# Turning q and k on VectorE in 32x32 blocks, with x2 kept by every fourth column

## Chip, cores and metric

The kernel runs on one core of one Trainium2 chip. The metric is the device time of one execution in microseconds (us); lower is better. Of the kernel before there are three times, 2680.54, 2680.54 and 2683.51 us; their median is 2680.54 us.

## The reference, cut to what matters

Two layers over 2048 tokens of width 1024, all in float32. Layer A normalises x, projects it to [u | z], pools u over 2, 4, 8 or 16 trailing tokens, maps and gates it, projects it back, and adds a gated embedding; its result is called x2 below. From x2 come the shared keys and values, and layer B's queries and gate:

```python
kv_in = rms_norm(x, kv_norm)
k_all, v_all = jnp.split(kv_in @ w_kv, 2, axis=-1)
k_sh = rms_norm(split_heads(k_all), k_norm)       # 16 heads of 64
v_sh = split_heads(v_all)
h = rms_norm(x, b_norm[j])
q, z = jnp.split(h @ b_w_in[j], 2, axis=-1)
q = rms_norm(split_heads(q), b_q_norm[j])
o = stick_breaking_attention(q, k_sh, v_sh)
x = x + (o * jax.nn.silu(z)) @ b_w_out[j]
```

For a query t and an earlier key s the weight is `beta[t,s] * prod_{s<j<t} (1 - beta[t,j])` with `beta = sigmoid(q.k / 8)`; only keys before t count. The kernel uses that the weights are differences of a running product, so it multiplies the running product with differences of neighbouring values, v[t-1] - v[t].

## The kernel before, in words

Every float32 operand of a product is split into a high and a low part, and a product is three matmuls: high x high, high x low, low x high. The stream is kept with channels on the 128 partitions and tokens in the free dimension, in four chunks of 512 tokens (`NSUB`, `W5`).

**First stage** (lines 219 to 865). For each chunk 22 steps run in a written order (`steps`, L757 on): four times z and u of layer A (`run_z`, `run_u`), four output steps (`run_o`), four gate steps (`run_g`), and then two steps each for q, k and v (`run_kvq`, eight heads a step). Each step also fetches the weights two steps ahead and converts those of the next step (`Weights.fetch`, `Weights.convert`: high part on ScalarE L148, low part on VectorE L149). `run_g` makes x2 and its two parts with `split` (L589), stores both in DRAM, and squares x2 on ScalarE (L596); the sum of squares gives, by a matmul with a column of ones (L625), the norm of each token.

A q, k or v step has two halves of two token tiles (128 tokens each). In `run_kvq` x2 is the stationary operand, so the result (L614) has tokens on the partitions and eight heads in the free dimension. `keyed` scales it and takes each head's norm (ScalarE L710, L712, VectorE L714, GpSimd L80, L81); `normed` applies the norm (VectorE L722). When all four token tiles are done, four closures `finish(m)`, one for a pair of heads, are appended to `lag` and run in the next step, at the last k-tile of its first half (L618): four TensorE transposes against the identity (L731) bring a pair to channels on the partitions, in PSUM; ScalarE and VectorE split it (L737, or with the gain of q and k L739, L740), and one DMA stores it as `kd` or `qd` (L742).

For v, `token_major` makes a copy moved down by one partition with DMAs issued on ScalarE's queue (L664 to L674), since the token before lies on the partition before; the first row comes from the tile before, or from the chunk before through `ve`. `differences` subtracts on GpSimd (L691), splits, and stores to `vd` (L698). For the last chunk's second v step the DMAs go out on SyncE, and this work runs inside the attention (`early`).

`tc.keep_in_program_order` (named `stay` in places) fixes an instruction's place on its engine; `queue` (L88) does that for stores and loads on SyncE's queue; functions in `pend` run at the third k-tile of the next product (`stored_late`). Tiles come from pools with a fixed number of buffers: for example `t4` has four, shared by `hl`, `vv` and the kept weights.

**Second stage** (from L868): attention, last chunk first, one head after another, over key chunks from the last to the first ("slots"; `slots` L1211). In a slot TensorE multiplies q and k (`front`, L936, L937: two matmuls, of q as (high, low) and of q as (low, high) with the two parts of k below each other), ScalarE takes the sigmoid (L940), VectorE scans (L945, L948), TensorE turns the result (`turn`, L961), ScalarE and VectorE split it (L964, L965), and TensorE multiplies with v (`gather`, L973, L974). The loads of a slot (`load_q`, `load_k`, `load_v`) are issued one slot ahead (`begin(i + 1)`, L1253). In between, single matmuls of other work are laid into TensorE's order as fillers, their number a slot from a small estimate of VectorE's and TensorE's times (`shares`): during the last chunk's attention the gates z of all chunks (`gate_z`, whose products are scaled on VectorE by L1057), later the output projections (`post`).

Of the kernel before, what the change touches and what calls it, by code (L numbers as in the profile page):

```python
# [15 lines left out]
P = 128  # L16
# [19 lines left out]
def trunk_kernel(ctx, tc, x, xt, pt0, wut, cols, heads, zin, grp, aout, agate, aple,  # L36
# [22 lines left out]
    gqk = cp.tile([P, 1], F32, name="gqk")  # L59
# [7 lines left out]
    qd = [[dram.tile([P, 2, W5], F32, name=f"qd{s}_{m}") for m in range(NH // 2)] for s in range(NSUB)]  # L67
    kd = [[dram.tile([P, 2, W5], F32, name=f"kd{s}_{m}") for m in range(NH // 2)] for s in range(NSUB)]
    vd = [[dram.tile([8, P, 4, P], F32, name=f"vd{s}_{b}") for b in range(2)] for s in range(NSUB)]
# [116 lines left out]

    def load_q(c, h):
        qa = io.tile([P, W5], F32R, tag="io", name="qa")
        qb = io.tile([P, W5], F32R, tag="io", name="qb")
        rows = qd[c][h // 2][h % 2 * HD : (h % 2 + 1) * HD]  # L190
        for l in range(2):
            nc.sync.dma_start(out=f(qa)[l * HD : (l + 1) * HD], in_=rows[:, l])
            nc.sync.dma_start(out=f(qb)[(1 - l) * HD : (2 - l) * HD], in_=rows[:, l])
        return qa, qb

    def load_k(kc, h):
        kk = io.tile([P, W5], F32R, tag="io", name="kk")
        rows = kd[kc][h // 2][h % 2 * HD : (h % 2 + 1) * HD]
        for l in range(2):
            nc.sync.dma_start(out=f(kk)[l * HD : (l + 1) * HD], in_=rows[:, l])  # L200
        return kk

    def load_v(kc, h):
        vv = io.tile([P, 4, P], F32R, tag="io", name="vv")
        nc.sync.dma_start(out=f(vv), in_=vd[kc][h // 8][h % 8])
        return vv
# [12 lines left out]
    with ExitStack() as st:  # L219
# [17 lines left out]
        hp = st.enter_context(tc.tile_pool(name="hp", bufs=1))  # L237
        halo = [[hp.tile([P, HALO], F32, name=f"halo{o}_{i}") for i in range(2)] for o in range(KT)]
# [15 lines left out]
        def split(pr, src, lo):  # L254
            A.copy(out=pr[:, 0], in_=src)
            lo.tensor_tensor(out=pr[:, 1], in0=src, in1=f(pr[:, 0]), op=ALU.subtract)

# [234 lines left out]
        def run_u(s, g, wu):  # L492
# [7 lines left out]
            for k in range(2):  # L500
                o = 2 * g + k
                ub = t2.tile([P, HALO + W5], F32, tag="ub", name="ub", bufs=2)
# [3 lines left out]
                cur, lo, sh = ub, 0, 1  # L506
                while sh < win:
                    nx = t2.tile([P, HALO + W5], F32, tag="us", name="us", bufs=2)
# [62 lines left out]
        def run_g(s, b, wg, wl):  # L571
# [13 lines left out]
            for k in range(2):  # L585
# [3 lines left out]
                split(pr, t, V)  # L589
# [3 lines left out]
            for k in range(2):  # L593
                o, t = 2 * b + k, ts[k]
                sq = tmp("sq")
                A.activation(out=sq, in_=t, func=AF.Square)  # L596
# [6 lines left out]
        def run_kvq(s, kind, b, ws):  # L603
            ck = chunk[s]
            for j0 in (0, 2):
# [25 lines left out]
                fins = [token_major(s, kind, b, j0 + i, pss2[i]) for i in range(2)]  # L631
# [16 lines left out]
        def token_major(s, kind, b, j, ps):  # L648
            tk = slice(j * P, (j + 1) * P)
            rj = chunk[s]["r2"][:, j : j + 1]  # L650
            ps8 = ps.rearrange("q (h d) -> q h d", d=HD)
            if kind == "v":

                if s == NSUB - 1 and b:
                    both = f(pair("vl"))
                    vr, vs = (both[:, e].rearrange("q (h d) -> q h d", d=HD) for e in range(2))
                else:
                    vr = t2.tile([P, 8, HD], F32, tag="tmp", name="vr", bufs=8)
                    vs = t2.tile([P, 8, HD], F32, tag="qn", name="vs", bufs=5)
                A.activation(out=vr, in_=ps8, func=AF.Identity, scale=rj)  # L660
                last = s == NSUB - 1 and b
                start = nc.sync.dma_start if last else nc.scalar.dma_start
                prev, chunk[s]["vr"] = chunk[s].get("vr"), vr
                start(out=ve[s][b][j : j + 1], in_=vr.rearrange("q h d -> q (h d)")[P - 1 : P])  # L664

                def shifted(stay=lambda ins: ins):
# [673 lines left out]
```

## Time and profile before

| | |
|---|---|
| median of three times | 2680.54 us |
| time of the profiled execution's span (first to last instruction) | 2679.3 us |
| VectorE, ScalarE, GpSimd busy | 71%, 52%, 35% |
| DMA | 590 MB, 220 GB/s on average |
| q1, the queue of SyncE: share of the 16 DMA engines' span | 65.3% |
| TensorE clock granted | 1.000 |

The profiled execution's own time is its span of 2679.3 us and about 1.2 us around it, 2680.5 us. PE is TensorE's matmul row, PEld its weight loads, DVE is VectorE, ACT ScalarE, POOL GpSimd, SP SyncE. A row "out<-in" names tiles by the program's names; a mean time of a matmul is longer than the distance to the next one, since matmuls are pipelined. A line number is that of the listing above.

### The profile page before, as it was taken

The numbers are of one execution on the slowest core, as the hardware profiler recorded it, in microseconds if no ns is written. First come the engines' busy times: TensorE is split into PE (matmuls) and PEld (weight loads), VectorE is DVE, ScalarE is ACT, GpSimd is POOL, SyncE is SP. The second block draws the span as 40 slices with busy tenths as digits, with TensorE's granted clock in tenths as the row PEclk, the third lists the DMA queues.
The fourth block names the chain that finished last, engine by engine and source line by source line (L and its number), as shares of the span: only waits on it lengthen the run. The fifth ranks groups of instructions, "written<-read, shape, count | busy, mean of one in ns | idle before, by whom it ended". The sixth has DMA issues, their size and how long they took to land.

```text
span 2679.3 us, 39424 instructions
## 1 busy us (share of the span) xinstructions
PE 2668.1 (100%) x13358; PEld 2229.9 (83%) x13358; DVE 1911.5 (71%) x2474; ACT 1397.2 (52%) x2735; POOL 927.7 (35%) x740
## 2 busy tenths in 40 slices
PE   9999999999999999999999999999999999999999
PEld 7888888888888888888888888888888888888887
DVE  6776625665266643665399999999999998886632
ACT  6455623455135551345356666666666666665531
POOL 2675337643486434853221111122111221212220
PEclk9999999999999999999999999999999999999999
DMA  8657795567856678543679665556766677778975
GB/s 327 222 175 271 251 308 188 192 240 251 303 175 226 232 259 298 168 151 134 223 236 286 195 220 176 166 172 191 211 199 177 185 222 227 201 209 261 267 237 177
DMA packets 281366, 590.00 MB, mean 220 GB/s; under 512 B 33702, under 2 KB 67750, under 8 KB 281164
## 3 DMA queue, kind: packets, MB, share of 16 engines
q1 hardware_dynamic: 270818, 571.41, 65.3%
q0 software_dynamic: 4608, 8.39, 1.9%
q10 hardware_dynamic: 5738, 7.68, 1.0%
q8 instruction: 106, 1.74, 0.3%
q14 instruction: 96, 0.79, 0.1%
HBM read 438.40 MB, written 136.38 MB: 215 GB/s over the span
## 4 chain that ended last, share of the span: by engine, by line
PE 97%; DVE 1%; DMA 0%; issue 0%; ACT 0%; SPq 0%; ACTq 0%; DVEq 0%
PE psd L614 19%; PE psd L168 9%; PE psd L167 9%; PE psd L166 9%; PE psa L961 9%; PE psd L1023 6%; PE psd L1025 6%; PE psd L1027 6%; PE pso L974 5%; PE psl L937 5%; PE pso L973 5%; PE psl L936 5%; PE pst L731 1%; PE psdt L1023 1%; PE psdt L1025 1%; PE psdt L1027 1%
## 5 line engine op out<-in xcount | busy, mean ns | idle before, releaser
L614 PE MATMUL psd<-wpair,x 128*128 128x512 f32 x2304 | 536.8, 391 | 0.0
L948 DVE TENSOR_TENSOR_SCAN pp<-kap,pp,zeros 128x512 f32<-128x512 f32 x384 | 513.5, 1339 | 7.7 <-ACT kap L940 7.0
L964 ACT CAST at<-psa 128x512 fp32r<-128x512 f32 (+3 forms) x640 | 325.7, 523 | 348.6 <-PE psa L961 338.1
L614 PEld LDWEIGHTS psd<-wpair,x 128*128 128x128 f32 x2304 | 429.9, 188 | 87.0
L965 DVE TENSOR_TENSOR at<-psa,at 128x512 fp32r<-128x512 f32 (+3 forms) x640 | 375.1, 598 | 62.0 <-ACT at L964 57.5
L940 ACT ACTIVATE kap<-psl 128x512 f32<-128x512 f32 (+3 forms) x640 | 345.7, 540 | 94.0 <-PE psl L937 90.6
L961 PE MATMUL psa<-ident,pp 128*128 128x128 f32 x2176 | 329.4, 273 | 2.0 <-DVE at L965 1.5
L961 PEld LDWEIGHTS psa<-ident,pp 128*128 128x128 f32 x2176 | 263.6, 140 | 58.2 <-DVE at L965 4.2
L936 PE MATMUL psl<-kk,qa 128*128 128x512 f32 (+3 forms) x640 | 275.1, 430 | 0.5 <-ACT at L964 0.5
L945 DVE TENSOR_TENSOR_SCAN pp<-kap,ahead 128x128 f32<-128x128 f32 (+3 forms) x256 | 224.3, 878 | 40.1 <-ACT kap L940 38.7
L974 PE MATMUL pso<-at,vv 128*128 128x512 f32 (+3 forms) x640 | 234.0, 366 | 0.0
L937 PE MATMUL psl<-kk,qb 128*128 128x512 f32 (+3 forms) x640 | 232.9, 364 | 0.0
L973 PE MATMUL pso<-at,vv 128*128 128x512 f32 (+3 forms) x640 | 232.3, 363 | 0.0
L167 PE MATMUL psd<-xp,wpair 128*128 128x512 f32 x512 | 199.5, 390 | 2.0 <-DVE xp L316 2.0
L166 PE MATMUL psd<-xp,wpair 128*128 128x512 f32 x512 | 199.8, 391 | 1.1 <-ACT xp L315 1.1
L168 PE MATMUL psd<-xp,wpair 128*128 128x512 f32 x512 | 199.3, 390 | 0.0
L149 DVE SCALAR_TENSOR_TENSOR wpair<-wraw,gains,wpair 128x512 fp32r<-128x512 f32 x192 | 161.7, 883 | 46.1 <-ACT wpair L148 45.6
L143 POOL TENSOR_TENSOR wpair<-wraw,wpair 128x512 fp32r<-128x512 f32 x99 | 145.5, 1479 | 82.0 <-ACT wpair L141 78.1
L148 ACT ACTIVATE wpair<-wraw,gains 128x512 fp32r<-128x512 f32 x192 | 132.9, 718 | 64.2 <-DMA wraw<-in_bq_dram 25.9
L141 ACT CAST wpair<-wraw 128x512 fp32r<-128x512 f32 x148 | 89.9, 618 | 121.4 <-PE psd L168 87.5
L1062 POOL TENSOR_TENSOR zr<-zr,sgz 128x512 f32<-128x512 f32 x32 | 61.6, 1924 | 257.3 <-ACT sgz L1061 233.8
L974 PEld LDWEIGHTS pso<-at,vv 128*128 128x128 f32 x640 | 120.2, 188 | 26.3
(207 smaller groups left out, 5338.9 us busy)
## 6 DMA issues: line engine op xcount, KB each, us to landing
kk<-kd SPq DMA_DIRECT2D x320, 128.0 KB
vv<-vd SPq DMA_DIRECT2D x160, 256.0 KB
wraw<-in_kv_dram SPq DMA_DIRECT2D x128, 256.0 KB
wpair<-wzd SPq DMA_DIRECT2D x64, 512.0 KB
wpair<-wod SPq DMA_DIRECT2D x64, 512.0 KB
wpair<-wgd SPq DMA_DIRECT2D x64, 512.0 KB
wpair<-wu SPq DMA_DIRECT2D x48, 512.0 KB
wpair<-wi SPq DMA_DIRECT2D x36, 512.0 KB
```

What stands on the lines that cost most here:

```text
L166: T.matmul(ps, wst(units, kt, 0, c0), acts[kt][:, 0], start=(begin and kt == order[0]), stop=False)
L167: T.matmul(ps, wst(units, kt, 0, c0), acts[kt][:, 1], start=False, stop=False)
L168: T.matmul(ps, wst(units, kt, 1, c0), acts[kt][:, 0], start=False, stop=(end and kt == order[-1]))
L614: T.matmul(pss2[i], ck["x2"][kt][:, xh, tk], wst(ws, kt, wh, 0, W5), start=(kt == 0 and xh == 0 and wh == 0), stop=(kt == KT - 1 and wh == 1))
L936: T.matmul(ps[:, :w], qa[:, qs], kk[:, :w], start=True, stop=False)
L937: T.matmul(ps[:, :w], qb[:, qs], kk[:, :w], start=False, stop=True)
L940: A.activation(out=kp[:, r0:], in_=ps[:, :w], func=AF.Sigmoid, scale=-1.0)
L948: V.tensor_tensor_scan(out=pp[:, ::-1], data0=kp[:, ::-1], data1=zeros.to_broadcast([P, W5]), initial=st["carry"][j], op0=ALU.mult, op1=AL ...
L961: T.transpose(pt[:, j * P : (j + 1) * P], pp[:, r0 + kt * P : r0 + (kt + 1) * P], ident)
L965: V.tensor_tensor(out=at[:, 1, cs], in0=pt[:, cs], in1=f(at[:, 0, cs]), op=ALU.subtract)
L973: T.matmul(po[:, cs], vv[:, kt, :], at[:, 0, cs], start=(st["diag"] and kt == 0), stop=False)
L974: T.matmul(po[:, cs], vv[:, kt, :], at[:, 1, cs], start=False, stop=(st["last"] and kt == 3))
```

## The change

Four things, which belong together:

- **x2 by fours.** `run_g` writes the parts of x2 with every fourth column together (`by_four`): column j*128 + t of the tile is token 4t + j. A token tile j of a q, k or v step then holds tokens j, 4 + j, 8 + j and so on, one per partition. The square of x2 is permuted alike. The gate z undoes the order when it is scaled (L1057), and x2 itself is stored as before.
- **Block transposes.** `normed` scales in place and then lets VectorE turn each 32x32 block of the tile (`V.transpose`) into a buffer `blocks`, written with a step of four elements. A quadrant of 32 partitions then holds 128 consecutive tokens, and the partition in it is a channel of 32. The four TensorE transposes of `finish` go; the split reads `blocks` in SBUF. `blocks` shares its memory with the pooling's work tiles, which become one tile `work`.
- **Layout in DRAM.** q and k are stored as the blocks lie, with channels in another order (the same for q and k); q is stored twice, as (high, low) and (low, high), with three DMAs, one DMA for k. The stores go through `pend`. q, k and v are each loaded by one DMA of 128 partitions, four pieces of 512 bytes a partition: two DMAs for the two forms of q, where there were four, and one for k, where there were two.
- **v.** Token 4t + j - 1 lies on the same partition of the tile before, so only tile 0 needs a shifted copy (of tile 3), and the other three subtract in place.

```diff
+        def by_four(pr, src, lo):
+            src = src.rearrange("q (t j) -> q j t", j=4)
+            A.copy(out=fours(pr[:, 0]), in_=src)
+            lo.tensor_tensor(out=fours(pr[:, 1]), in0=src, in1=fours(f(pr[:, 0])), op=ALU.subtract)
...
-                split(pr, t, V)
+                by_four(pr, t, V)
...
-                A.activation(out=sq, in_=t, func=AF.Square)
+                A.activation(out=fours(sq), in_=t.rearrange("q (t j) -> q j t", j=4), func=AF.Square)
...
-            qn = t2.tile([P, 8, HD], F32, tag="qn", name="qn", bufs=5)
             tc.keep_in_program_order(
-                V.tensor_tensor(out=qn, in0=qs, in1=rq.unsqueeze(2).to_broadcast([P, 8, HD]), op=ALU.mult))
+                V.tensor_tensor(out=qs, in0=qs, in1=rq.unsqueeze(2).to_broadcast([P, 8, HD]), op=ALU.mult))
+            tc.keep_in_program_order(
+                V.transpose(out=blocks[:, :, :, j], in_=qs.rearrange("q h (g t) -> q (h g) t", t=32)))
...
-                pt = turned()
-                for i in range(4):
-                    ins = T.transpose(pt[:, i, :], rows[i][:, 2 * m : 2 * m + 2, :].rearrange("q h d -> q (h d)"), ident)
...
-                if kind == "k":
-                    split(hl, pt, V)
+                src = blocks[:, 4 * m : 4 * m + 4].rearrange("q (e g) t j -> q e g (t j)", e=2)
+                hi, lo = hl[:, :, 0], hl[:, :, 1]
+                if kind == "k":
+                    A.copy(out=hi, in_=src)
+                    V.tensor_tensor(out=lo, in0=src, in1=f(hi), op=ALU.subtract)
...
+                    for g in range(2):
+                        A.activation(out=hi[:, :, g], in_=src[:, :, g], func=AF.Identity, scale=gqk[:, g : g + 1])
+                        V.scalar_tensor_tensor(out=lo[:, :, g], in0=src[:, :, g], scalar=gqk[:, g : g + 1],
+                                               in1=f(hi[:, :, g]), op0=ALU.mult, op1=ALU.subtract)
...
-                queue(out=(kd if kind == "k" else qd)[s][4 * b + m], in_=f(hl))
+                    queue(out=qa.rearrange("e a (p x) n -> (a p) e (x n)", x=4), in_=whole)
+                    for l in range(2):
+                        queue(out=qb.rearrange("e a (p l g) n -> l (a p) e (g n)", l=2, g=2)[l],
+                              in_=f(hl)[:, :, 1 - l].rearrange("q e g n -> q e (g n)"))
+                pend.append(store)
...
+        nc.sync.dma_start(out=f(rows), in_=src.rearrange("a r n -> r a n"))
...
-                    for lo, hi in ((0, 112), (112, P - 1)):
-                        stay(start(out=vs[lo + 1 : hi + 1], in_=vr[lo:hi]))
-                    if j:
-                        stay(start(out=vs[0:1], in_=prev[P - 1 : P]))
+                fins = [lambda: differences(s, b, j, vrs[j - 1][0], vr, vs)]
+                if j == 3:
+                        for lo, hi in ((0, 112), (112, P - 1)):
+                            stay(start(out=vs0[lo + 1 : hi + 1], in_=vr[lo:hi]))
...
-                V.tensor_tensor(out=zr, in0=ps, in1=rb, op=ALU.mult)
+                V.tensor_tensor(out=zr.rearrange("q (t j) -> q t j", j=4), in0=ps.rearrange("q (j t) -> q t j", j=4),
+                                in1=rb.rearrange("q (t j) -> q t j", j=4), op=ALU.mult)
```

More of the change, by code (lines that the diff above doesn't have):

```diff
@@ L648, in token_major @@
         def token_major(s, kind, b, j, ps):
-            tk = slice(j * P, (j + 1) * P)
             rj = chunk[s]["r2"][:, j : j + 1]
@@ L657, in token_major @@
                 else:
-                    vr = t2.tile([P, 8, HD], F32, tag="tmp", name="vr", bufs=8)
-                    vs = t2.tile([P, 8, HD], F32, tag="qn", name="vs", bufs=5)
+                    vr, vs = t2.tile([P, 8, HD], F32, tag="tmp", name="vr", bufs=8), None
                 A.activation(out=vr, in_=ps8, func=AF.Identity, scale=rj)
-                last = s == NSUB - 1 and b
-                start = nc.sync.dma_start if last else nc.scalar.dma_start
-                prev, chunk[s]["vr"] = chunk[s].get("vr"), vr
@@ L676, in token_major @@
[L676 to L683 removed]
+                vrs = chunk[s].setdefault(("v", b), [])
+                vrs.append((vr, vs))
+                if not j:
+                    return []
+                fins = [lambda: differences(s, b, j, vrs[j - 1][0], vr, vs)]
```

104 lines of the change are left out of this document (52 added, 52 removed).

## The prediction

> **What bounds the kernel now.** I read the page first, then the chain of waits in order of time.
>
> ```profile
> span 2679.3 us, 39424 instructions
> ...
> PE 2668.1 (100%) x13358; PEld 2229.9 (83%) x13358; DVE 1911.5 (71%) x2474; ACT 1397.2 (52%) x2735; POOL 927.7 (35%) x740
> ...
> PE 97%; DVE 1%; DMA 0%; issue 0%; ACT 0%; SPq 0%; ACTq 0%; DVEq 0%
> PE psd L614 19%; PE psd L168 9%; PE psd L167 9%; PE psd L166 9%; PE psa L961 9%; PE psd L1023 6%; PE psd L1025 6%; PE psd L1027 6%; PE pso L974 5%; PE psl L937 5%; PE pso L973 5%; PE psl L936 5%; PE pst L731 1%; PE psdt L1023 1%; PE psdt L1025 1%; PE psdt L1027 1%
> ```
>
> TensorE is idle for 11 us of 2679.3, and 97% of the chain that ended last is its own instruction order. A microsecond of TensorE work that disappears is therefore a microsecond of time, unless another engine is close behind at that place. The change deletes one of the lines in the chain, L731 (the transposes of q and k). Its price has to be read from pace, not from busy time, because matmuls are pipelined. These are pieces of the chain (start, length, work):
>
> ```profile
> 219.93 10.88 PE psd L614 x48
> 230.81 0.79 PE pst L625 x8
> ...
> 277.14 0.87 PE pst L731 x8
> ...
> 300.80 0.87 PE pst L731 x8
> ...
> 328.01 31.08 PE psd L614 x137
> ```
>
> The eight transposes at 277.14 and at 300.80 stand at the same place of two neighbouring steps (k, first and second half of the heads), so one step with transposes takes 23.66 us. A step has 96 matmuls of L614 (2 halves, 8 k-tiles, 2 token tiles, 3 products); at the pace of the stretch that holds nothing else, 31.08/137 = 0.2269 us each, they take 21.78 us. The other 1.88 us are the 16 transposes of the step and what the change between the two kinds of matmul costs. The form-by-form list has these rows (busy us, mean ns of one, idle before):
>
> ```profile
> L965 DVE TENSOR_TENSOR at<-psa,at 128x512 fp32r<-128x512 f32 x448 | 301.8, 679 | 51.1 <-ACT at L964 46.9
> ...
> L731 PE MATMUL pst<-ident,qn 128*128 128x128 f32 x256 | 36.4, 275 | 0.2
> ...
> L256 DVE TENSOR_TENSOR x<-tx,x 128x512 fp32r<-128x512 f32 x32 | 35.1, 1126 | 3.1 <-ACT x L255 3.1
> ...
> L965 DVE TENSOR_TENSOR at<-psa,at 128x256 fp32r<-128x256 f32 x64 | 26.0, 406 | 9.4 <-ACT at L964 9.1
> ...
> L740 DVE SCALAR_TENSOR_TENSOR hl<-pst,gqk,hl 128x512 fp32r<-128x512 f32 x32 | 22.4, 743 | 0.0
> ...
> L1057 DVE TENSOR_TENSOR zr<-psd,rb 128x512 f32<-128x512 f32 x32 | 21.4, 668 | 0.1
> L256 DVE TENSOR_TENSOR hl<-pst,hl 128x512 fp32r<-128x512 f32 x32 | 21.2, 685 | 16.1 <-ACT hl L255 16.0
> ...
> L149 DVE SCALAR_TENSOR_TENSOR wpair<-wraw,g_a,wpair 128x256 fp32r<-128x256 f32 x24 | 13.7, 605 | 0.3 <-ACT wpair L148 0.2
> ```
>
> **The change, part by part.** *TensorE.* All 256 transposes go: 16 steps x 1.88 us = 30.1 us. Nothing is added on TensorE; every other matmul keeps its shape and its contiguous operands. This is the one term on the path for certain.
>
> *VectorE in the q and k steps.* Each step gains four block transposes of 128x512. None is in the trace. The nearest rows are a one-pass instruction of that size, 0.67 us (L1057), and a scan of it:
>
> ```profile
> L948 DVE TENSOR_TENSOR_SCAN pp<-kap,pp,zeros 128x512 f32<-128x512 f32 x384 | 513.5, 1339 | 7.7 <-ACT kap L940 7.0
> ```
>
> So 2.7 to 5.4 us a step; I take 1.0 us each, 4 us, since the writing is strided. The low halves now read SBUF twice instead of PSUM once: for k 4 x (1126 - 685) ns = 1.8 us, for q eight half-size instructions, 8 x 605 - 4 x 743 ns = 1.9 us. What a step has today, and other stretches used below (window, then busy time of PE, PEld, DVE, ACT, POOL, clock, DMA share, GB/s):
>
> ```profile
> 219.00:328.00 109.00, 108.96 (x517) 90.39 (x516) 69.22 (x103) 64.12 (x112) 43.90 (x41) 1.00 0.68 245
> 267.00:278.00 11.00, 11.00 (x54) 9.23 (x53) 5.44 (x9) 6.03 (x11) 4.04 (x4) 1.00 0.65 248
> 278.00:290.00 12.00, 12.00 (x59) 9.79 (x58) 9.84 (x18) 8.86 (x18) 4.04 (x4) 1.00 0.81 281
> ...
> 1337.00:1450.00 113.00, 112.34 (x610) 93.48 (x608) 107.23 (x124) 68.06 (x136) 21.02 (x13) 1.00 0.86 260
> 1450.00:1600.00 150.00, 149.89 (x832) 125.65 (x833) 146.62 (x175) 98.94 (x197) 21.65 (x14) 1.00 0.70 212
> 1600.00:1750.00 150.00, 149.86 (x839) 125.96 (x838) 146.25 (x176) 98.30 (x199) 22.53 (x14) 1.00 0.57 179
> 1750.00:1900.00 150.00, 149.85 (x833) 125.41 (x832) 146.98 (x174) 102.28 (x207) 37.81 (x22) 1.00 0.63 187
> 1900.00:2200.00 300.00, 299.03 (x1663) 251.45 (x1662) 282.87 (x348) 199.82 (x414) 54.58 (x38) 1.00 0.69 195
> 2200.00:2400.00 200.00, 200.00 (x1106) 171.20 (x1105) 174.13 (x226) 127.08 (x279) 39.71 (x27) 1.00 0.75 214
> 2400.00:2600.00 200.00, 199.41 (x1039) 168.42 (x1038) 115.92 (x181) 100.52 (x242) 49.55 (x37) 1.00 0.85 254
> ```
>
> VectorE is busy 5.44 + 9.84 = 15.3 us in a step today; afterwards 15.3 + 1.9 + 4 = 21.2 us (19.9 to 22.6) of a step that has shrunk to 21.8 us. That is tight, so its cover has to be named: TensorE waits for VectorE here only through the converted weights.
>
> ```profile
> 223.20 1.28 DVE L256 TENSOR_TENSOR x<-tx,x 128x512 fp32r<-128x512 f32 x2
> ...
> 285.91 2.07 DVE L149 SCALAR_TENSOR_TENSOR wpair<-wraw,gains,wpair 128x512 fp32r<-128x512 f32 x3
> ```
>
> The three conversions at 285.91 are the sixth to eighth weight tile of the step that starts at 300.80 - 10.9 = 289.9. The first of them is ready at 286.6 and used after five k-tiles, 30 matmuls or 6.8 us into the step, at 296.7: 10 us early. Even at the upper end VectorE falls behind by 0.8 us a step, 3 us over the four q and k steps of a chunk, and the v steps behind them have none of the new work. Cost 0; without that cover it would be one for one.
>
> The new waits. ScalarE's high-half copies wait for VectorE's block transposes where they waited for TensorE's; behind them on ScalarE stands the reading of the step's own products (L710), whose PSUM tiles are six, two for each half step of 10.9 us, so TensorE would notice after two halves. The single block buffer makes a step's first block transpose wait for the previous step's last halves; those stand ahead of it on VectorE anyway. Stores of q and k wait for the next half step (SyncE no longer blocks on them at once), and their four buffers, which the kept weights and v share, stay taken some 4 us longer; the next user comes a half step later. Cost 0.
>
> *x2 by fours.* 32 copies and 32 squares on ScalarE and 32 subtractions on VectorE read every fourth column. No row of the trace has such a stride. Below: as now. Above: the streaming part doubles; by L965, 679 - 406 = 273 ns for 256 elements, 0.55 us more for 512 (taken for ScalarE too). Where it could reach TensorE is the start of a chunk's q steps. The last two low halves end at 224.48 and are first used after six k-tiles, 36 matmuls, at 228.1. The sum of squares behind them:
>
> ```profile
> 223.35 3.98 POOL L599 TENSOR_TENSOR acc<-acc,sq 128x512 f32<-128x512 f32 x2 [3.75 <-ACT sq L596]
> ```
>
> It ends at 227.33 and is wanted by L625 at 230.81. Each has 3.5 us of slack against at most four operations, 2.2 us. Cost 0.
>
> *zr.* The 32 products of L1057 read PSUM at a stride of 512 bytes. They run at 1340 to 1885 us, beside the last chunk's attention, where VectorE is 95 to 98% busy. Bounds as above: 0, or 32 x 0.55 = 17.6 us more VectorE time against 5.8 + 3.4 + 3.8 + 3.0 = 16 us of idle time in the four windows 1337 to 1900. With half of the idle time usable, 9 us reach the path; I take 0 for the sum, because nothing in the trace shows a stride to cost anything, and keep 9 for a rival (bounds 2 to 17).
>
> *Loads.* k, q and v now come as 512-byte pieces. What a piece costs, from the DMA view of 290 to 302 us (weights, 2 and 4 KB rows) and of 350 to 362 us, where v is stored in 3290 - 218 = 3072 pieces of 512 bytes:
>
> ```profile
> q1 hardware_dynamic: 1322, 2.66, 58.2%
> ```
> ```profile
> DMA packets 3814, 3.20 MB, mean 267 GB/s; under 512 B 218, under 2 KB 3290, under 8 KB 3814
> ...
> q1 hardware_dynamic: 3430, 2.67, 70.2%
> ```
>
> First window: 58.2% of 16 engines x 12 us = 112 us for 2.66 MB, 42 us a MB, 86 ns for 2 KB. Second: 135 us, less 1.10 MB of long rows at 42 us, leaves 89 us or 29 ns a piece, 115 ns for four. The Trainium skill (DMA: Bandwidth & Descriptors, Specifications) puts line rate at 512 bytes and up; by that rule four pieces would cost the same 86 ns and the loads nothing, and the trace disagrees, 115 against 86.
>
> ```profile
> kk<-kd SPq DMA_DIRECT2D x320, 128.0 KB
> vv<-vd SPq DMA_DIRECT2D x160, 256.0 KB
> ...
> qa<-qd SPq DMA_DIRECT2D x128, 128.0 KB
> qb<-qd SPq DMA_DIRECT2D x128, 128.0 KB
> ```
>
> These are 57,344 rows of 2 KB: 57,344 x 29 ns / 16 = 104 us over the 1340 us of attention, 0.08 more DMA share. The fullest stages go from 0.85 and 0.86 to 0.94. Not over 1, so cost 0; SyncE issues 288 loads fewer. In the q steps the second copy of q adds 4 MB a chunk, 4.2 x 42 / 16 = 11 us of 16 engines to the 109 us at share 0.68 (0.78), while most v shifts go. Cost 0, under that cover.
>
> *v shifts.* Fewer DMAs on ScalarE's queue, less waiting on GpSimd, which isn't in the chain: 0.
>
> Sum: -30.1 us. On the profiled execution, 2679.3 + 1.2 outside the span = 2680.5, which is also the median shown: **2650 us**. 0.2%, 5 us, is about what a measurement of this kernel can tell from no change.
>
> **The rivals.**
> *Strides cost* (zr doubles): 2650 + 9 = 2659, from 2652 to 2667. For it: no stride in the trace says otherwise, and VectorE has 2% left there. Against: the other windows of attention need VectorE less, and fillers can shift. The Trainium skill states the rule (SBUF — State Buffer, Door 1: The DMA port swizzle): each access that moves to a new line of 16 bytes in SBUF, or 8 in PSUM, pays. No row of this trace can show it.
>
> *512-byte loads are dear* (the other side). The 29 ns are from stores; loads in scattered pieces may cost more. The share rises by (4p - 86) x 57,344 / 16 / 1340 us for a price of p ns; at p = 46 that is 0.26, so 1337 to 1450 us becomes 1.12, 2200 to 2400 1.01 and 2400 to 2600 1.11: 14 + 2 + 22 = 38 us lost, 2688 us. It cancels the gain from 45 ns on. Against: DMA has 0% of the chain now, and each load is issued a whole slot ahead (L1253), so that landing some tenths of a us later changes nothing while the share stays under 1.
>
> *VectorE becomes the bound of q and k steps.* A step has 21.8 - 17.2 = 4.6 us for its four block transposes, 1.15 us each; the 10 us of slack spread over a chunk's sixteen add 0.6, so TensorE waits from 1.8 us each on. At 2.3 us it would be (4 x 2.3 + 17.2 - 21.8) x 4 - 10 = 8.4 us a chunk, 34 in all: 2684. For it: the writing is strided. Against: 2.3 us is 1.7 times the scan.
>
> *The room is given back elsewhere* (weights in the shorter steps come late at DMA shares over 0.8): about 2678, no change.
>
> **How the numbers follow.** Forecast 0.58 (own range 2645 to 2655), strides 0.27, dear loads 0.06, VectorE 0.04, given back 0.05. The range 2644 to 2664 holds the forecast and most of the strides' case. Faster 0.87 (forecast, strides, some of the last), same 0.04, slower 0.09.
>
> **What would show it.** Right: no L731 on PE, q and k steps 21.8 us apart, idle PE time unchanged near 11 us, block transposes near 1 us, zr near 0.67 us. Strides: zr and the x2 subtractions about 0.5 us longer, VectorE idle under 1% at 1340 to 1885 us, PE waiting there. Dear loads: DMA share near 1 late in attention, PE waiting for kk or vv. Wrong altogether: the steps keep their 23.7 us.

## The result and the profile after

The changed kernel takes 2653.13 us (median of four runs, 2652.24 to 2653.59), the kernel before 2680.88 us in the same series (2680.54 to 2683.51): ratio 0.9895 with a 95% interval of 0.9881 to 0.9909. That is 27.8 us less; the forecast was 2650, with 2644 to 2664 as the range. The page of the changed kernel, its span and busy times, and the first line of its chain:

```profile
span 2651.8 us, 38568 instructions
...
PE 2640.3 (100%) x13102; PEld 2205.3 (83%) x13102; DVE 1984.8 (75%) x2570; ACT 1427.5 (54%) x2767; POOL 939.8 (35%) x740
...
PE 89%; DMA 3%; DVE 2%; POOL 2%; ACT 2%; issue 1%; SPq 0%; ACTq 0%; DVEq 0%; POOLq 0%
```

TensorE has 256 instructions less, its idle time is still 11 us, and it is still the bound. But its own order holds only 89% of the chain where it held 97%: at more places something else ends last by a hair. Two stretches of the chain show what a chunk's q, k and v steps have become (start, length, work):

```profile
232.91 120.25 PE psd L619 x528
...
550.33 119.80 PE psd L619 x528
```

528 matmuls in 119.80 us are 0.2269 us each, with nothing between them; the first chunk's stretch is 0.45 us longer. The trace's first and last matmul of each chunk's q, k and v steps give the gain by stage: these steps shrink by 6.2, 7.7, 6.1 and 7.7 us in chunks 0 to 3, while the other steps of the first stage and attention keep their time to within 0.8 us. The first q step starts 0.3 us later. So chunks 1 and 3 get the full gain, and chunks 0 and 2 lose about 1.5 us of it each. The form-by-form list of the changed kernel (busy us, mean ns of one, idle before):

```profile
L734 DVE STREAM_TRANSPOSE work<-qs 128x512 f32<-128x512 f32 x64 | 70.1, 1095 | 0.9
L732 DVE TENSOR_TENSOR qs<-qs,rq 128x512 f32<-128x512 f32 x64 | 49.7, 777 | 44.8 <-POOL rq L81 44.8
L260 DVE TENSOR_TENSOR x<-tx,x 128x512 fp32r<-128x512 f32 x32 | 44.8, 1414 | 13.1 <-ACT x L259 13.1
L601 ACT ACTIVATE sq<-tx 128x512 f32<-128x512 f32 x32 | 35.9, 1132 | 0.0
...
L259 ACT CAST x<-tx 128x512 fp32r<-128x512 f32 x32 | 35.2, 1108 | 6.0 <-DVE tx L589 6.0
L747 ACT ACTIVATE hl<-work,gqk 128x256 fp32r<-128x256 f32 x64 | 26.5, 497 | 54.9 <-DVE work L734 54.9
L748 DVE SCALAR_TENSOR_TENSOR hl<-work,gqk,hl 128x256 fp32r<-128x256 f32 x64 | 26.3, 483 | 4.6 <-ACT hl L747 3.5 <-DMA wraw<-in_kv_dram 1.2
L1077 DVE TENSOR_TENSOR zr<-psd,rb 128x512 f32<-128x512 f32 x32 | 21.4, 668 | 0.1
...
L744 DVE TENSOR_TENSOR hl<-work,hl 128x512 fp32r<-128x512 f32 x32 | 20.2, 685 | 4.1 <-ACT hl L743 4.1
L743 ACT CAST hl<-work 128x512 fp32r<-128x512 f32 x32 | 17.8, 618 | 64.3 <-DVE work L734 64.3
```

The block transpose (L734) takes 1.095 us. zr (L1077), which reads PSUM at a stride of 512 bytes, takes the same 668 ns as before. The copy of x2 (L259) and its square (L601) on ScalarE, which read SBUF at a stride of 16 bytes, take 1108 and 1132 ns; they took 614 and 626:

```profile
L596 ACT ACTIVATE sq<-tx 128x512 f32<-128x512 f32 x32 | 19.8, 626 | 0.0
...
L255 ACT CAST x<-tx 128x512 fp32r<-128x512 f32 x32 | 19.4, 614 | 8.9 <-DVE tx L584 8.8
```

And ScalarE waits 119 us in all for block transposes (the idle columns of L743 and L747). The windows of the changed kernel, at the same places as before the change (columns as in the prediction):

```profile
219.00:328.00 109.00, 108.45 (x480) 88.81 (x479) 87.47 (x125) 64.91 (x117) 51.12 (x44) 1.00 0.88 301
1310.00:1423.00 113.00, 112.12 (x608) 93.16 (x606) 107.08 (x124) 67.94 (x134) 21.80 (x13) 1.00 0.85 270
...
2373.00:2573.00 200.00, 199.93 (x1042) 169.04 (x1041) 116.08 (x182) 100.75 (x242) 49.92 (x38) 1.00 0.82 255
```

In the first of these windows, which holds the q and k steps of chunk 0 and the start of its v steps, VectorE is now busy 87 of 109 us (69 before) and the DMA engines 0.88 (0.68 before). In attention the DMA share has not risen: 0.85 and 0.82, where it was 0.86 and 0.85.

### The profile page after: what moved, and what is told of

Same layout as the page of the kernel before. It is cut to its first block, busy times and chain, and to the rows that moved or that the text cites. A ratio compares the mean times of both kernels' runs of the same rounds, so it can differ in the third digit from the quotient of the medians.

```text
span 2651.8 us, 38568 instructions
## 1 busy us (share of the span) xinstructions
PE 2640.3 (100%) x13102; PEld 2205.3 (83%) x13102; DVE 1984.8 (75%) x2570; ACT 1427.5 (54%) x2767; POOL 939.8 (35%) x740
## 4 chain that ended last, share of the span: by engine, by line
PE 89%; DMA 3%; DVE 2%; POOL 2%; ACT 2%; issue 1%; SPq 0%; ACTq 0%; DVEq 0%; POOLq 0%
PE psd L619 16%; PE psa L981 9%; PE psd L166 8%; PE psd L167 8%; PE psd L168 8%; PE psd L1043 6%; PE psd L1045 6%; PE psd L1047 6%; PE pso L994 5%; PE psl L957 5%; PE pso L993 5%; PE psl L956 5%; DMA wraw<-in_bq_dram 1%; PE psdt L1043 1%; PE psdt L1045 1%
## 5 line engine op out<-in xcount | busy, mean ns | idle before, releaser
L619 PE MATMUL psd<-wpair,x 128*128 128x512 f32 x2304 | 525.6, 390 | 1.4 <-DVE wpair L149 0.8
L149 DVE SCALAR_TENSOR_TENSOR wpair<-wraw,gains,wpair 128x512 fp32r<-128x512 f32 x192 | 164.8, 891 | 31.9 <-ACT wpair L148 30.9
L148 ACT ACTIVATE wpair<-wraw,gains 128x512 fp32r<-128x512 f32 x192 | 129.7, 716 | 47.4 <-DMA wraw<-in_bq_dram 35.6
```

The lines of the kernel that those rows point to most:

```text
L619: T.matmul(pss2[i], ck["x2"][kt][:, xh, tk], wst(ws, kt, wh, 0, W5), start=(kt == 0 and xh == 0 and wh == 0), stop=(kt == KT - 1 and wh == 1))
```

## The experiments

Each run stands beside runs of the kernel before on its own chip (2680.7 to 2680.8 us). The line numbers of the first stage move by a few lines from kernel to kernel.

**The transposes put back** (pe_back).

```diff
             def finish(m):
+                pt = turned()
+                for i in range(4):
+                    T.transpose(pt[:, i, :], ident, ident)
                 hl = ...
```

> The changed kernel with 256 TensorE transposes of the identity, four at the head of each finish(m), at the place of the removed ones; nothing reads them. Theory (the gain is TensorE's own time): 16 steps x 1.88 us come back, 2653 + 30 = 2683 us, slightly above the kernel before, because the 2.6 us that the changed kernel lost of its gain stay lost or are partly covered (2680 to 2684). Rival (the gain comes from the new loads and the fewer DMAs): the transposes find room beside other waits, 2653 to 2660.

Measured: 2679.73 us (2678.66 to 2683.58), ratio 0.9995 [0.9985, 1.0004]. The order of TensorE's other instructions is the same as in the changed kernel, so 256 transposes on TensorE are worth 26.6 us there, nearly the whole gain. In the profiled execution, at 2683.58 us the slowest of the ten, they cost more than their own time: once TensorE waits for the sums of squares (the chain), and behind it runs at half its clock (0.50 in the window's PEclk column). The steps of chunk 1 are 4.5 us longer there than in the kernel before. The other nine took 2678.66 to 2679.98 us, so the 26.6 us hardly hold that wait.

```profile
554.85 1.60 POOL acc L604
556.45 0.04 issue
556.50 1.46 PE pst L630 x8
```
```profile
559.40:562.80 3.40, 3.40 (x10) 2.63 (x9) 1.34 (x2) 3.02 (x5) 1.12 (x3) 0.50 1.00 369
```

**The transposes taken away and nothing else** (before_no_turn). In the kernel before, the halves are made from the token rows as they are.

```diff
-                pt = turned()
-                for i in range(4):
-                    ins = T.transpose(pt[:, i, :], rows[i][...], ident)
-                    ...
-                pt = pt.rearrange("q j t -> q (j t)")
+                pt = rows[m].rearrange("q h d -> q (h d)")
```

> The kernel before without its 256 transposes; the split reads a token tile as it lies, so q and k are not turned and the scores mean nothing. Theory: 2680.9 - 30.1 = 2651 us, and at most 1 us of it lost, since VectorE has no block transposes and ScalarE does not wait for them: 2650 to 2652, some 2 us under the changed kernel. Rival (deleting the transposes alone brings little, the rest of the change is needed): above 2665.

Measured: 2685.02 us (2682.06 to 2686.47), ratio 1.0014 [1.0005, 1.0023]. A miss: with less work it was no faster. The removal had changed more than I meant. A copy that needs only row m runs earlier than one that needs all four, and without the transposes nothing held ScalarE's copies in their place. So it was repeated with rows[3] for all four splits and the copies kept in their order (before_no_turn2).

> The kernel before without its transposes, q and k not turned, as in before_no_turn, but all four splits of a step read the last token tile and their ScalarE copies keep their place in the order; without that the first two ran a half step early, and SyncE and ScalarE blocked on them (weights 3 us late in the k steps, and the clock at half for 3 to 10 us behind each wait). Theory (deleting the transposes is the whole gain): 2650 to 2653 us. Rival (the transposes gave the other engines time that they need, so that without the rest of the change the room is lost again): above 2665.

Measured: 2679.45 us (2676.27 to 2680.49), ratio 0.9993 [0.9983, 1.0002]. The rival held. The q, k and v steps do shrink, by 7.1, 6.2, 5.7 and 7.7 us, but nearly all of it is lost again right behind them, at the second step of the next chunk. These are the loads and stores on SyncE's queue and then TensorE, in the kernel before:

```profile
352.94 9.03 SPq L90 DMA_DIRECT2D vd<-vv  x4
362.07 6.69 SPq L90 DMA_DIRECT2D wpair<-wu  x4
```
```profile
370.17 0.48 PE L166 MATMUL psd<-xp,wpair 128*128 128x512 f32 x1
```

and the same in before_no_turn2:

```profile
352.90 10.06 SPq L90 DMA_DIRECT2D vd<-vv  x4
363.05 6.71 SPq L90 DMA_DIRECT2D wpair<-wu  x4
```
```profile
363.07 0.60 PE L246 MATMUL pst<-ident,rx 128*128 128x128 f32 x4
369.51 0.77 PE L166 MATMUL psd<-xp,wpair 128*128 128x512 f32 x1 [5.84 <-DMA wpair<-wu]
```
```profile
366.80:373.60 6.80, 4.09 (x10) 3.25 (x11) 0.69 (x1) 0.62 (x1) 1.28 (x1) 0.50 1.03 361
```

In both, SyncE comes to the weights wu only at 362 to 363 us, because four stores of v stand ahead of them. TensorE comes to wu 6.7 us earlier without the transposes, and waits. The chain puts 6.33 us from this issue to the landing. In the kernel before, the trace's semaphore records show the first of these weights landed at 368.4 us, and they are used at 370.17: 1.8 us to spare, of which no row of waits says anything until it is gone. TensorE 6.7 us earlier and wu issued 1.0 us later make that -5.9 us; 5.84 us is what TensorE waits. Then its clock is at 0.50 for 6.8 us. A wait of that size stands in all three chunks that have a next one (6.1, 7.9 and 7.2 us between two starts of matmuls that should be 0.4 apart). In the second and third of them more went than the shorter steps took: 3.4 and 3.3 us were to spare before, and counted from the chunk's first q matmul wu is issued 3.5 and 3.3 us later than in the kernel before. Why it is later there stays open. The first version (before_no_turn) has these three waits as well (6.5, 5.8 and 4.9 us), and three of 1.9 to 3.5 us inside the q, k and v steps. What holds the stores of v are the shifted copies, which they need (the two runs with and without them, below, test this): the part of the change that I had priced at nothing.

**The same without the v shifts** (no_turn_no_shift).

```diff
-                else:
+                elif not j:
                     shifted()
-                return lambda: differences(s, b, j, vr, vs)
+                return lambda: differences(s, b, j, vs if last or not j else prev, vr, vs)
...
-            stay(G.tensor_tensor(out=vs, in0=vs, in1=vr, op=ALU.subtract))
+            stay(G.tensor_tensor(out=vs, in0=vp, in1=vr, op=ALU.subtract))
```

> The kernel before without the 256 transposes (the halves are made from unturned rows, as in before_no_turn2) and with the differences of v taken straight from the tile of the row before, so that only the first of each four rows of v is shifted through DMA; the values of q, k and v are not the reference's. No block transposes, no strides. Theory S: the waits of 6 to 8 us at the first z or u step of three chunks go, and 2649 to 2654 us are left, 26 to 32 us under before. Rival T: the waits stay, 2674 to 2681 us as in before_no_turn2 (2679.45).

Measured: 2650.17 us (2649.31 to 2650.85), ratio 0.9883 [0.9868, 0.9898]. Theory S held (its range was 2649 to 2654): three of four shifts fewer bring 29.3 us, once the transposes are gone. SyncE's queue and the chain of this kernel:

```profile
347.56 6.38 SPq L90 DMA_DIRECT2D vd<-vv  x4
354.04 3.72 SPq L90 DMA_DIRECT2D wpair<-wu  x4
```
```profile
549.36 119.80 PE psd L614 x528
```

wu is issued 9 us earlier than with the shifts (before_no_turn2). The steps shrink by 7.7 us in every chunk, and from 100 us to the end of the first stage no two matmuls of TensorE start more than 0.7 us apart. This is what removing the transposes brings when nothing else gets in the way: 30.6 us.

**The shifts put back into the changed kernel** (after_shifts).

```diff
                     vr, vs = t2.tile([P, 8, HD], F32, tag="tmp", name="vr", bufs=8), None
+                    if j:
+                        vs = t2.tile([P, 8, HD], F32, tag="qn", name="vs", bufs=5)
...
+                    for lo, hi in ((0, 112), (112, P - 1)):
+                        nc.scalar.dma_start(out=vs[lo + 1 : hi + 1], in_=vr[lo:hi])
+                    nc.scalar.dma_start(out=vs[0:1], in_=vrs[j - 1][0][P - 1 : P])
+                    fins = [lambda: differences(s, b, j, vs, vr, vs)]
```

> The changed kernel in which rows 1 to 3 of each v step get their row above as before the change: three shifted copies through DMA into vs, for every v step except the last chunk's second. (With the changed token order this takes the wrong neighbour, so the values of v are not the reference's; the work is that of before.) Theory S, the fewer v shifts keep the gain: the stores of v wait on SyncE for the shifted copies, the weights of the next chunk's z and u steps queue behind them, and TensorE waits 5 to 8 us at the first of these steps in three chunks with half the clock for about as long behind it: 2670 to 2680 us. Rival T, the shifts have no part and the removed transposes alone bring the gain: 2652 to 2656 us and no TensorE wait over 2 us at the first z or u step of a chunk.

Measured: 2687.82 us (2685.92 to 2689.61), ratio 1.0025 [1.0015, 1.0034]. The mechanism is that of theory S, but 34.7 us are lost, 8 us more than the upper end of its range. The chain at the first chunk's end, then TensorE:

```profile
350.22 4.12 DMA vs<-vr
358.38 4.25 DMA vs<-vr
365.99 6.42 DMA wpair<-wu
```
```profile
372.56 0.77 PE L166 MATMUL psd<-xp,wpair 128*128 128x512 f32 x1 [7.02 <-DMA wpair<-wu]
```

Between the lines shown stand subtractions on GpSimd and copies on ScalarE: shifted copy, subtraction, ScalarE, shifted copy, subtraction, halves, the store's issue, weights, TensorE. The waits at the three places (7.3, 10.5 and 9.0 us from one start to the next) are some 26 us of the 34.7; half the clock behind each and smaller waits make the rest. So the changed kernel with all its shifts is slower than the kernel before. With the fewer shifts the margin at this place is no wider, but it moves with TensorE: in the changed kernel wu is issued 6.4 us before its use in all three chunks and lands 1.2 to 1.4 us before it, and with the transposes back (pe_back) it is issued 6.4 us before its use too, though that use comes 5 to 23 us later.

**Every block transpose twice** (twice).

```diff
             tc.keep_in_program_order(
                 V.transpose(out=blocks[:, :, :, j], in_=qs...))
+            tc.keep_in_program_order(
+                V.transpose(out=blocks[:, :, :, j], in_=qs...))
```

> The changed kernel with every block transpose done twice, the second time onto the same place: 4 x 1.10 us more VectorE time in each of the 16 q and k steps. Theory (the cover of the weights is used up: the last weight tiles of the first v step are ready 0.1 us before their use): VectorE has about 19.5 us of a 21.8 us step, becomes 23.9, 2 us a step over, 6 to 9 us a chunk lost, 2677 to 2690 us. Rival (the cover of 10 us from the prediction still stands): 4 x 2.1 - 10 is below nothing, 2653 to 2656.

Measured: 2664.63 us (2662.84 to 2665.79), ratio 0.9937 [0.9922, 0.9952], between the two ranges, so that neither theory's time came. 70 us more of VectorE cost 11.5 us of time: part of it finds cover. ScalarE's waits for the block transposes grow from 119 to 152 us:

```profile
ACT hl L745 <- DVE work L736: 82.9, 8, 12.5
ACT hl L749 <- DVE work L736: 68.9, 8, 12.0
```

and TensorE waits for weights (L148 on ScalarE, L149 on VectorE) at seven places, 0.8 to 2.4 us from one start to the next. The loss lies in the q, k and v steps of the first three chunks (4.9, 4.8 and 1.5 us); the fourth, which has no steps of a next chunk beside it, loses nothing.

**Block transposes that write in order** (dense_blocks).

```diff
-                V.transpose(out=blocks[:, :, :, j], in_=...
+                V.transpose(out=dense_blocks[:, j], in_=...
```

> The changed kernel, the block transposes writing their columns side by side and not every fourth, so that q and k are in the wrong order. Theory (the stride of 16 bytes is what costs 1.10 us): 0.65 to 0.72 us each, 4 x 0.4 = 1.6 us less VectorE a step, weights ready about 5 us earlier in the first v step, the 1 us wait of the third chunk gone: 2651 to 2653 us. Rival (a block transpose of float32 costs 1.1 us by itself): 1.10 us, time as the changed kernel.

Measured: 2650.15 us (2649.94 to 2651.0), ratio 0.9886 [0.9872, 0.9901]. The transpose takes 706 ns where it took 1095:

```profile
L735 DVE STREAM_TRANSPOSE work<-qs 128x512 f32<-128x512 f32 x64 | 45.2, 706 | 0.5
```

Each chunk's steps now shrink by 7.6 to 7.7 us, and in the same stretch no two starts are more than 0.7 us apart. So the 3.0 us that the changed kernel misses to no_turn_no_shift go to the stride with which its block transposes write: 64 x 389 ns = 25 us of VectorE.

**x2 read in order and written at a stride** of 512 bytes (write_stride): is the price of the x2 permutation one of reading?

```diff
-            src = src.rearrange("q (t j) -> q j t", j=4)
+            src = src.rearrange("q (t j) -> q t j", j=4)
...
-            return ap.rearrange("q (j t) -> q j t", j=4)
+            return ap.rearrange("q (j t) -> q t j", j=4)
```

> The changed kernel; the copies, squares and subtractions of x2 read the columns in order and write with a stride of 512 bytes, to the same layout. Theory A (a read at a stride of 16 bytes or more is what doubled the copy from 0.62 to 1.11 us, a write is free): copy and square back near 0.63 us, the subtraction between 0.7 and 1.1 since its second operand is read at the stride; the 0.7 us wait of TensorE at the start of the first chunk's q step goes, 2651 to 2653 us. Theory B (either side pays): copy and square stay at 1.1 us, time 2653.

Measured: 2655.09 us (2654.07 to 2656.62), ratio 0.9903 [0.9888, 0.9918]. Theory A fell, and B held for the price: on ScalarE a write at a stride of 512 bytes is as dear as a read at a stride of 16. VectorE's subtraction reads one operand and writes at the stride in this run, so it does not tell the two apart. The time is 2.0 us above the changed kernel's, which B had not forecast; in chunk 2 TensorE waits for the sum of squares (1.4 us between two starts).

```profile
L260 DVE TENSOR_TENSOR x<-tx,x 128x512 fp32r<-128x512 f32 x32 | 48.0, 1519 | 12.6 <-ACT x L259 12.6
L601 ACT ACTIVATE sq<-tx 128x512 f32<-128x512 f32 x32 | 36.6, 1163 | 0.0
...
L259 ACT CAST x<-tx 128x512 fp32r<-128x512 f32 x32 | 35.8, 1137 | 5.7 <-DVE tx L589 5.6
```

**One stored form of q** (one_q): are the missing microseconds the DMA share of 0.88?

```diff
-                    for l in range(2):
-                        queue(out=qb..., in_=...)
...
-        load_rows(qd[c][h // 2][i][h % 2], nm)
+        load_rows(qd[c][h // 2][0][h % 2], nm)
```

> The changed kernel without the second stored form of q (both loads of q take the first form, so the scores are wrong). 16.8 MB less in the q and k steps. Theory A (VectorE's backlog is what uses up the cover of the weights): the last weight tiles of the first v step still about 0 to 1 us ahead of their use, time 2652 to 2654. Theory B (the DMA share of 0.88 in these steps delays the raw weights): share about 0.78, weights 3 us or more ahead, the wait of the third chunk gone, 2651 to 2652.

Measured: 2652.47 us (2652.12 to 2652.75), ratio 0.9894 [0.988, 0.9909], 0.7 us under the changed kernel, less than a measurement tells. In the window of 219 to 328 us the DMA share falls from 0.88 to 0.74, and still a wait for weights (1.6 us between two starts) stands in chunk 0, whose steps shrink by 5.7 us, less than in the changed kernel. In chunk 2 the wait is gone, as theory B said (7.6 us instead of 6.1). So the second store of q may have a part in where the waits fall; the larger part is VectorE's backlog, as dense_blocks shows.

**Each load in two DMAs of 64 partitions** (half_loads).

```diff
-        nc.sync.dma_start(out=f(rows), in_=src.rearrange("a r n -> r a n"))
+        for l in range(2):
+            nc.sync.dma_start(out=f(rows)[l * HD : (l + 1) * HD], in_=src.rearrange("a r n -> r a n")[l * HD : (l + 1) * HD])
```

> The changed kernel, each load of q, k and v as two DMAs of 64 partitions, still in pieces of 512 bytes. Theory (a DMA onto 64 partitions is served more slowly than one onto 128, which is why the DMA share of the attention did not rise by the forecast 0.08): the share of 2373 to 2573 us rises from 0.82 to 0.88 or more, time still 2653 since nothing waits. Rival (128 or 64 partitions is the same and 512-byte pieces simply cost a quarter of 2 KB): share 0.82, time 2653.

Measured: 2675.76 us (2672.25 to 2678.13), ratio 0.9981 [0.9972, 0.9991]. Neither theory had this, and the run is not a clean test. Two of its windows:

```profile
1310.00:1423.00 113.00, 111.98 (x611) 93.31 (x611) 106.69 (x124) 68.83 (x136) 21.80 (x13) 1.00 0.84 244
...
2373.00:2573.00 200.00, 185.85 (x957) 155.61 (x956) 116.42 (x175) 96.89 (x237) 47.62 (x34) 0.98 0.78 228
```

Until 2423 us nothing is lost: TensorE comes to that place 1.0 us earlier than in the changed kernel. In the window from 2373 us on TensorE is idle for 14 of 200 us, with the DMA engines at 0.78. From 2423 to 2556 us, and only there, the program gives TensorE's instructions another order than the changed kernel does (fillers of the output projection stand elsewhere), so the loss can't be put down to the loads. What set the new order stays open. What the run does show is that twice as many loads of half the size cost nothing in the 1070 us of attention before 2373 us.

**Two attempts at a better version.** Both write the squares of x2 in order (the norm's matmul then picks every fourth column) and keep five raw weight buffers instead of three; the second also subtracts the low halves of k on GpSimd.

```diff
-                A.activation(out=fours(sq), in_=t.rearrange("q (t j) -> q j t", j=4), func=AF.Square)
+                A.activation(out=sq, in_=t, func=AF.Square)
...
-  tc.tile_pool(name="wraw", bufs=3)
+  tc.tile_pool(name="wraw", bufs=5)
...
-                    V.tensor_tensor(out=lo, in0=src, in1=f(hi), op=ALU.subtract)
+                    G.tensor_tensor(out=lo, in0=src, in1=f(hi), op=ALU.subtract)
```

> The changed kernel with the squares of x2 written in order (the norm's matmul picks every fourth column instead) and with five raw weight buffers instead of three. It computes the reference. If the 2.6 us that are missing from 30.1 are ScalarE's and VectorE's backlog at the head of the first q and v steps of chunks 0 and 2, the two TensorE waits of about 1 us shrink: 2650 to 2652.5 us. If it is the order of the queues there and not the amount, no difference: 2653 to 2654 us.

> The kernel of both, with the 32 low halves of k (22 us of VectorE in all) subtracted on GpSimd. It computes the reference. Theory, VectorE's backlog in the q and k steps: as with the contiguous block transposes (25 us of VectorE less, 2650.15) 2649.5 to 2651.5 us, no TensorE wait over 0.7 us in the q, k and v steps. Rival, GpSimd in its turn makes the sums of squares and the differences of v late: 2654 to 2665 us.

Measured: 2676.09 us (2672.57 to 2680.93), ratio 0.9981 [0.9972, 0.999], and 2680.28 us (2677.24 to 2682.92), ratio 0.9998 [0.9989, 1.0007]. Both missed, and for a reason that none of the theories had. The waits of the first one in its profiled execution (2680.93 us, the slowest of eleven), 160 to 183 us, before any square is taken:

```profile
PE psd L166 <- ACT x L250: 7.3, 1, 7.3
ACT kpair L250 <- DMA kraw<-in_bout_dram: 7.3, 1, 7.3
```

ScalarE stands at the conversion of a weight that has not landed, and the split of an activation (x), which TensorE needs, is queued behind it. In the changed kernel that load was issued at 163.0 us, here at 169.5, though the order of the instructions on SyncE's queue is the same. Since no square has been taken by then, the five buffers are the suspect; neither edit was run alone, so this is argued, not shown. In the second one the low halves of k take 1418 ns on GpSimd, and waits for weights (1.0 to 2.0 us between two starts) remain in three chunks, so taking 22 us off VectorE in this way did not remove them.

## Why the prediction was right, and where it was not

**The transposes: right.** The sum took 16 x 1.88 = 30.1 us from the distance of two steps. With every cover in place (no_turn_no_shift) it is 30.6 us, 7.7 us or 4 x 1.93 a chunk.

**The v shifts: wrong, though the total came out.** The prediction priced "fewer v shifts" at 0. That edit was not run alone in the kernel before; pe_back, which has it together with transposes on TensorE, stands 1.1 us under the kernel before, so that 0 is near. But it is the cover of the first term: without it the gain is 1.2 us (before_no_turn2), with it 30.6. The step that failed is "Nothing is added on TensorE" taken as sufficient. I should have asked at each place behind the shortened steps what is late next once TensorE comes 7.5 us sooner. I asked it of the weights inside the q steps (10 us early) and not of the first steps of the next chunk, where the SyncE row for wu stood in the trace of before. The rival "the room is given back elsewhere, weights come late", at 2678, is the kernel before_no_turn2, 2679.45, to 1.5 us. It had 0.05, and what rules it out is the edit that I had called worthless. That this edit was part of the change at all is luck, as far as the forecast goes.

**VectorE in the q and k steps: the block transpose near, the low halves too dear, the cover wrong.** 1.0 us for a block transpose (bounds 0.67 to 1.34) measured 1.095. Of the low halves I expected 1126 ns for k and 605 for q, and they take 685 and 483. The 1126 ns had been taken for what reading SBUF twice costs, but that mean hides two kinds of instruction, as the view by line (shortest, median, longest) of the kernel before shows:

```profile
L256 DVE TENSOR_TENSOR x<-tx,x x32: 678/693/1789, 182.1 to 1196.9; 128x512 fp32r<-128x512 f32 x32
```

The usual one takes about 0.69 us (18 of the 32 take under 0.7), and 11 take 1.8 us; what makes these long was not tried. The 10 us of slack were not there at the end. ScalarE and VectorE in the first v step of chunk 2 of the changed kernel:

```profile
939.23 1.66 ACT L743 CAST hl<-work 128x512 fp32r<-128x512 f32 x3 [10.17 <-DVE work L734]
...
945.75 2.55 ACT L148 ACTIVATE wpair<-wraw,gains 128x512 fp32r<-128x512 f32 x4
```
```profile
949.36 1.77 DVE L732 TENSOR_TENSOR qs<-qs,rq 128x512 f32<-128x512 f32 x1 [0.51 <-POOL rq L81]
951.05 0.74 DVE L149 SCALAR_TENSOR_TENSOR wpair<-wraw,gains,wpair 128x512 fp32r<-128x512 f32 x1
```
```profile
951.85 0.97 PE L619 MATMUL psd<-wpair,x 128*128 128x512 f32 x3 [0.83 <-DVE wpair L149]
```

ScalarE is blocked 10.17 us behind the block transposes. Behind its copies stand not only L710, as I wrote, but also the weight conversions L148 of the next step, and behind these the low halves on VectorE. The new wait was named, but its queue was not listed in full. TensorE waits 0.83 us here. With shorter transposes the waits go (dense_blocks, 3.0 us better); with longer ones they grow (twice, 11.5 us worse).

**x2 by fours: size right on ScalarE, smaller on VectorE, slack not.** Estimated 0.55 us more for each operation, at most 2.2 us against 3.5 us of slack. Measured: 0.49 and 0.51 us on ScalarE. On VectorE the shortest of the subtractions went from 678 to 1073 ns, 0.40 us more, and their mean from 1126 to 1414, 0.29 us more. TensorE still waits 0.55 us for the last low half in the first chunk:

```profile
230.69 1.20 PE L619 MATMUL psd<-wpair,x 128*128 128x512 f32 x4 [0.55 <-DVE x L260]
```

The slack had been read as if all else stayed: the inputs of these operations came 4 us later than before, since raw weights landed later ahead of them on ScalarE and VectorE. Why those loads were later was not tried.

**zr and the strides' rival: fallen.** 668 ns before and after. The Trainium skill (SBUF — State Buffer, Specifications) gives lines of 16 bytes in SBUF, where each crossing to a new line pays, and of 8 bytes in PSUM. On SBUF the traces agree (614 to 1108 ns at a stride of 16 bytes); VectorE reading PSUM at a stride of 512 bytes, with every element in another line, pays nothing here. The forecast had taken 0 there only because no row spoke for a price, and the rival's 0.27 was fair for that state of knowledge.

**Loads: cost 0 right, the share wrong.** I worked out 0.08 more DMA share in attention from 29 ns a piece; in the two stages quoted it fell instead, by 0.01 and 0.03. The pieces' price was right: in the trace's packet records a 512-byte packet of these loads takes about 28 ns. What was wrong is the 86 ns for a 2 KB row: it came from a window of weight loads, and in the attention of before such packets last 116 ns on average (median 84), about four times 28. So "the trace disagrees, 115 against 86" compared two windows of different load and does not hold for these loads. The dear-loads rival falls with it. In the q steps 0.78 was forecast and 0.88 measured; without the second copy of q it is 0.74 (one_q), so that the copy takes 0.14 and not 0.10.

**VectorE as the bound:** it was given as a sharp threshold, nothing below 1.8 us a transpose. The three prices that were run show no such threshold: against 0.706 us (dense_blocks), 3.0 us are lost at 1.095 us already, and at 2.19 (twice) another 11.5, where the formula gives (4 x 2.19 + 17.2 - 21.8) x 4 - 10 = 6.6 us a chunk, 27 in all. The formula spreads a step's work evenly over the step, and the rows above show it bunched, with ScalarE blocked for 10 us behind it; that this is why there is no threshold is argued, not tested.

## What to carry to other kernels

Where an engine loses work, walk down its next wait at every later place and write down the margin of each, also where the profile of before shows no wait: here margins of 1.8 to 3.4 us, which no row of waits shows, decided over 29 us. An edit that is worth nothing alone can be the condition for another; price such parts of a change together, and test them apart in both directions. For a new wait, list everything that is queued behind it on its engine, weight conversions for later steps too.

## What the runs showed of the hardware

A short wait of TensorE can cost more than itself. In pe_back two matmuls start 2.0 us apart at 554.5 us, and behind that the granted clock is 0.50 in the window quoted above: ten matmuls in 3.40 us, where 15 fit at full speed. The distance alone does not decide it: after 1.9 us (twice, 318.0 us), 2.1 and 2.2 us (half_loads, 2497.6 and 2525.9 us) and 2.3 us (both, 1131.1 us) the clock stayed at 1.00, and after 2.4 us (twice, 337.1 us) it fell to 0.50. What else decides stays open. The Trainium skill (TensorE: Matmul & The Clock Gate, Part 1) puts the drop behind at least one idle window of about 3.4 us; here 2.0 us between two starts were enough once, while the stretches at 0.50 that followed had the page's length, 3.4 us (in the run twice), or double that (pe_back).

A block transpose of 128x512 in float32 on VectorE takes 706 ns when it writes in order (dense_blocks) and 1095 ns when it writes every fourth element (the changed kernel).
